# A gMLP trunk on one core: the second block's x is transposed by DMA in 16-bit planes, weights are asked for a unit sooner, and TensorE runs on the identity at the start

## Chip, core and metric

The kernel runs on one core of a Trainium2 chip. The metric is the device time in microseconds (us) of one execution, given as the median of three runs. The core's engines each have their own queue of instructions and meet through semaphores: TensorE (PE in the profile; its weight loads are PEld), VectorE (DVE), ScalarE (ACT), GpSimd (POOL) and SyncE (SP), which issues all DMAs of this kernel.

## The reference

One layer of the reference is used (DEPTH 1, so the chunked gMLP). x is 2048 rows of 1024 (T and D_MODEL), E is 2048, all float32:

```python
c_act = jax.nn.silu(c)
mod = c_act @ ada_w[0] + ada_b[0]
shift, scale, gate = jnp.split(mod, 3, axis=-1)
h = rmsnorm(x, norm_g[0]) * (1.0 + scale[:, None, :]) + shift[:, None, :]
u, v, z = jnp.split(h @ w_in, 3, axis=-1)
u = jax.nn.gelu(u)
v = layernorm(jax.nn.gelu(v), ln_g, ln_b)
v = v.reshape(bsz, seq // 128, 128, 8, 256)
v = jnp.einsum("hpq,bnqhc->bnphc", sp_w, v) + sp_b.T[None, None, :, :, None]
y = (u * v.reshape(bsz, seq, 2048) * jax.nn.silu(z)) @ w_out
x = x + gate[:, None, :] * y
return rmsnorm(x, final_g)
```

## The kernel before

**Products.** Each float32 product is made of three fp32r matmuls (`mm3`, L177): an operand is split into a high part (`hi`, `sh`; a cast on ScalarE, L168) and a low part (`lo`, `sl`; what is left, a subtraction on VectorE, L169), and hi*hi, hi*lo and lo*hi are summed in PSUM. The large products go by a scheme of Strassen's kind with seven products (p1 to p7) of half the size, from sums of quarters: S1 to S4 of h (`strassen_sums`), and differences of the weights' quarters (`Unit.weights`, L342), which VectorE makes in place in the raw weights (`sub`, L345).

**Stages.** The rows of x are worked in two blocks of 1024. For each block v is made first (groups of 4 row tiles, `project_v`), then the 16 units, u and z in turn, of 256 columns each (`project`, L957). A unit's raw weights are 1 MB in the single buffer `raw0` (u) or `raw1` (z), loaded by `Unit.load` (L298). A unit's products are twelve matmuls of 128x512 each. `after` (L938) is the work on a unit's results one unit later: the spatial mixing (`pmix`), the products of u, v and z, stores to `g_dram`.

**The start** (L723 on) computes the modulation from c (`mod_sum`: a sum on VectorE, then `pm` on TensorE), loads the first 512 rows of x as four chunks of 128, normalises each (`normalize_steps`: square on ScalarE, a small row `r_m` on VectorE, a power on GpSimd, a scaling `x<-x,r` on VectorE) and transposes it on TensorE against the identity (`psx`, L269). Then come the first products, step k by step k of the 1024 (`p` from L806 on), of weights wfv and wfu; for each k `modulate` (L252) and `put` make sh and sl.

**The second block's x** is prepared beside block 0, a tile of 128 rows at a time (`prepare_h`, L659), in 8 tiles: load into the one buffer `hx`, normalise, transpose on TensorE into PSUM (`psh`, 8 transposes of 128x128 a tile, 64 in all), modulate on ScalarE into `ht`, store to `h_dram`. `preparations` (L854) hands out these steps, one at each hook of `project_v` or two in each unit; `side` (L908) starts the second block's sums (`prepare_sums`: from h_dram to hs_dram) in units 6, 8, 10 and 12. `refill` (L692) loads both at the turn of the blocks.

**Order.** A scheduler orders the instructions of TensorE, GpSimd and SyncE by its own estimate; in the start the order of VectorE and ScalarE is as written. All DMAs stand in one queue on SyncE, which issues in order: one that waits for its buffer holds all behind it. c tiles (2 KB a partition) come from a pool of 15.

Of the kernel before, what the change touches and what calls it, by code (L numbers as in the profile page):

```python
# [9 lines left out]
F32 = mybir.dt.float32  # L10
F32R = mybir.dt.float32r
BF16 = mybir.dt.bfloat16
AF = mybir.ActivationFunctionType
ALU = mybir.AluOpType
PSUM = bass.MemoryType.PSUM
# [2 lines left out]
P = 128  # L18
# [4 lines left out]
def kernel(  # L23
# [33 lines left out]
    nc = tc.nc  # L57

    T, D = x.shape
# [6 lines left out]
    KD = D // P  # L66
# [591 lines left out]

    def prepare_h(tp):  # L659

        xt = vp.tile([P, D], F32, tag="hx", name=f"x_1_{tp}", bufs=1)
        t0 = TB + tp * P
        nc.sync.dma_start(xt, x[t0:t0 + P, :])
        yield
        normalize_x(xt, f"1_{tp}")
        yield
        for i in range(KD // 4):
            ps = aux_bank(f"psh_{tp}_{i}")
            ht = c_tile(f"ht_{tp}_{i}", (P, 4, P))
            for kk in range(4):  # L670
                k = 4 * i + kk
                nc.tensor.transpose(ps[:, kk * P:(kk + 1) * P], xt[:, k * P:(k + 1) * P], ident)
            for kk in range(4):
                modulate(ht[:, kk, :], ps[:, kk * P:(kk + 1) * P], 4 * i + kk)
            nc.sync.dma_start(h_dram[:, 4 * i:4 * i + 4, tp * P:(tp + 1) * P], ht)
        yield

    def prepare_sums(k):
# [44 lines left out]
    with tc.tile_pool(name="start", bufs=1) as st:  # L723
# [22 lines left out]
        firsts = [units[2 * j] for j in range(NF)]  # L746
        v0, v1 = groups[0]

        def take_a1(k):
            ps = transpose_half(xh, 0, k, acc_bank if k < 5 else aux_bank)  # L750
            t = s_slot(S4, k % KH, "hl"[k // KH], F32, f"a1_{k}")
            if k == 0:
                modulate(t, ps, k)
            elif k in (1, 3):
                nc.vector.tensor_copy(t, ps)
            else:
                nc.scalar.activation(t, ps, AF.Copy)
            a1.append(t)

        with tc.manual_schedule(engines={mybir.EngineType.DVE, mybir.EngineType.Activation}):  # L760
            *_, pm[0] = mod_sum(0, aws[0])
            mod_cols(cols, 0, pm[0])
            sums = mod_sum(1, aws[1])
            for ch, xt in enumerate(xh):
                norm = normalize_steps(xt, f"0_{ch}")
                next(norm)
                pm[1] = next(sums)
                next(norm)
            ws = [first_split(k, wf[k]) for k in range(2)]
            for k in range(5):  # L770
                take_a1(k)
                if k == 0:
                    put(0, A11, 0, a1[0])
            for k in range(KD):
                if k + 3 < KD:
                    aws[k + 3] = mod_load(st, k + 3)
# [77 lines left out]
    def preparations():  # L854

        ln = prepare_ln()
        next(ln)
        sp = [prepare_spatial(g) for g in range(2)]
        next(sp[0])
        yield  # L860
        next(ln, None)
        next(sp[0])
        next(sp[1])
        yield
        next(sp[0], None)
        next(sp[1])
        yield
        next(sp[1], None)
        hs = [prepare_h(tp) for tp in range(NCH)]
        next(hs[0])  # L870
        yield
        for tp in range(1, NCH + 1):
            next(hs[tp - 1])
            yield
            next(hs[tp - 1])
            if tp < NCH:
                next(hs[tp])
            yield
# [29 lines left out]
    def side(i):  # L908

        next(prep, None)  # L910
        if i in (6, 8, 10, 12):
            prepare_sums((6, 8, 10, 12).index(i))
        if 0 <= i - NU < KD:
            for db in range(NDB):
                prepare_gate(NDB * (i - NU) + db, gate_sum)
# [41 lines left out]
    def project(i, u, rest):  # L957
# [10 lines left out]
        if turn:  # L968
            w0.load(0, 0, "raw0")
            w0.load(0, 1, "v0")  # L970
        if i % NU:
            u.load()
            u.p1()
            change(A11)
            u.p5()
# [391 lines left out]
```

## Time and profile before

| what | value |
|---|---|
| median of 3 runs | 1337.66 us (1336.67 to 1340.08) |
| the profiled execution | 1340.57 us, span 1338.7 us |
| TensorE busy | 1310.6 us, 98%, 6078 matmuls and transposes |
| VectorE busy | 1077.9 us, 81% |
| ScalarE busy | 683.9 us, 51% |
| GpSimd busy | 26.3 us, 2% |
| DMA | 229.23 MB, mean 171 GB/s |

The span is the time between the first and the last instruction of the profiled execution; its own time is 1.9 us longer. A row of a timeline gives the start, the length, the engine, the line and the operation, with out<-in by the program's names; in brackets stands how long the engine had been idle and what released it. Matmuls are pipelined, so the time that one takes from TensorE is the step from its start to the next one's start, not its length. The clock granted to TensorE has two levels, 1.2 and 2.4 GHz.

### The profile page before, as it was taken

What the parts mean: (1) busy time and instruction counts of PE and PEld (TensorE: products, weight loads), DVE (VectorE), ACT (ScalarE), POOL (GpSimd) and SP (SyncE); (2) the same over time, 40 slices, a digit from 0 to 9 for tenths busy, and PEclk for the clock granted to TensorE, in tenths of its full rate; (3) what the DMA queues carried; (4) which work ended last, traced back from release to release, by engine and by line L of the source; (5) the groups of instructions that cost most, each with busy time, mean ns of one, the idle gap of its engine ahead of it and who ended that gap; (6) DMA issues with size and microseconds to landing.
All of it is one profiled execution on the core that took longest, in us unless ns stands there. A gap on an engine that the chain in (4) does not pass through costs nothing.

```text
span 1338.7 us, 17246 instructions
## 1 busy us (share of the span) xinstructions
PE 1310.6 (98%) x6078; PEld 1089.7 (81%) x6078; DVE 1077.9 (81%) x1801; ACT 683.9 (51%) x1177; POOL 26.3 (2%) x42
## 2 busy tenths in 40 slices
PE   5999999999999999999999999999999999999997
PEld 4878887878788888888888888888888888888886
DVE  6889988878889888977687889887799944757875
ACT  5775444757655546634345555445543434344553
POOL 0000001000000000000000000000000000000101
PEclk9999999999999999999999999999999999999999
DMA  9871655546566448532242445334338722235733
GB/s 317 265 268 63 221 190 196 162 159 214 192 217 216 166 140 289 197 129 107 95 157 91 157 153 185 133 120 133 123 118 305 268 95 94 95 119 204 259 110 126
DMA packets 156798, 229.23 MB, mean 171 GB/s; under 512 B 9188, under 2 KB 91172, under 8 KB 153384
## 3 DMA queue, kind: packets, MB, share of 16 engines
q1 hardware_dynamic: 156712, 228.14, 50.1%
q8 instruction: 47, 0.77, 0.2%
q14 instruction: 39, 0.32, 0.1%
HBM read 160.47 MB, written 67.64 MB: 170 GB/s over the span
## 4 chain that ended last, share of the span: by engine, by line
PE 89%; DVE 4%; DMA 3%; issue 1%; ACT 1%; POOL 0%; SPq 0%; POOLq 0%; DVEq 0%; ACTq 0%
PE po L178 8%; PE po L180 8%; PE po L179 8%; PE p_z L180 7%; PE p_z L178 7%; PE p_z L179 7%; PE p_u L178 6%; PE p_u L180 6%; PE p_u L179 6%; PE p_v L178 6%; PE p_v L180 6%; PE p_v L179 6%; PE pmix_u L557 4%; DMA raw_u<-in_gm_w_in_dram 2%; PE p L180 1%
## 5 line engine op out<-in xcount | busy, mean ns | idle before, releaser
L178 PE MATMUL p_v<-hi_p_v,sh 128*128 128x512 f32 x416 | 162.5, 391 | 1.6 <-DVE u_v L485 1.0
L179 PE MATMUL p_v<-lo_p_v,sh 128*128 128x512 f32 x416 | 162.3, 390 | 0.0
L180 PE MATMUL p_v<-hi_p_v,sl 128*128 128x512 f32 x416 | 162.2, 391 | 0.0
L180 PE MATMUL po<-hi_o,gl 128*128 128x512 f32 x416 | 161.9, 389 | 0.0
L178 PE MATMUL po<-hi_o,gh 128*128 128x512 f32 x416 | 161.8, 389 | 0.0
L179 PE MATMUL po<-lo_o,gh 128*128 128x512 f32 x416 | 161.8, 389 | 0.0
L168 ACT ACTIVATE hi_p_v<-b_v 128x512 fp32r<-128x512 f32 x104 | 65.2, 631 | 108.4 <-PE p_v L180 87.7
L168 ACT ACTIVATE gh<-gr 128x1024 fp32r<-128x1024 f32 x52 | 55.1, 1061 | 127.0 <-PE po L179 117.4
L169 DVE TENSOR_TENSOR gl<-gr,gh 128x1024 fp32r<-128x1024 f32 x52 | 63.9, 1228 | 59.3 <-ACT gh L168 59.1
L169 DVE TENSOR_TENSOR lo_p_v<-b_v,hi_p_v 128x512 fp32r<-128x512 f32 x104 | 70.2, 690 | 35.9 <-ACT hi_p_v L168 35.7
L178 PEld LDWEIGHTS p_v<-hi_p_v,sh 128*128 128x128 f32 x416 | 78.1, 188 | 19.3 <-DVE u_v L485 1.9
L180 PEld LDWEIGHTS po<-hi_o,gl 128*128 128x128 f32 x416 | 78.1, 188 | 16.6 <-DVE gl L169 0.3
L178 PEld LDWEIGHTS po<-hi_o,gh 128*128 128x128 f32 x416 | 78.1, 188 | 16.1
L179 PEld LDWEIGHTS p_v<-lo_p_v,sh 128*128 128x128 f32 x416 | 78.1, 188 | 16.1 <-DVE lo_p_v L169 0.2
L179 PEld LDWEIGHTS po<-lo_o,gh 128*128 128x128 f32 x416 | 78.1, 188 | 16.1
L180 PEld LDWEIGHTS p_v<-hi_p_v,sl 128*128 128x128 f32 x416 | 78.1, 188 | 16.0
L542 ACT ACTIVATE vn<-vn,lm,lr 128x256 f32<-128x256 f32 x128 | 67.9, 594 | 24.1 <-DMA vn<-v_dram 18.8
L180 PE MATMUL p_z<-sh,lo_p_z 128*128 128x512 f32 x192 | 75.9, 396 | 2.1 <-DVE lo_p_z L169 2.0
L178 PE MATMUL p_z<-sh,hi_p_z 128*128 128x512 f32 x192 | 75.5, 393 | 1.0 <-ACT hi_p_z L168 1.0
L179 PE MATMUL p_u<-sl,hi_p_u 128*128 128x512 f32 x196 | 76.3, 389 | 0.0
L178 PE MATMUL p_u<-sh,hi_p_u 128*128 128x512 f32 x196 | 76.2, 389 | 0.0
L180 PE MATMUL p_u<-sh,lo_p_u 128*128 128x512 f32 x196 | 76.2, 389 | 0.0
(244 smaller groups left out, 3103.1 us busy)
## 6 DMA issues: line engine op xcount, KB each, us to landing
gr<-g_dram SPq DMA_DIRECT2D x26, 1024.0 KB, 4.7
b_v<-in_gm_w_in_dram SPq DMA_DIRECT2D x18, 1024.0 KB, 7.5
vn<-v_dram SPq DMA_DIRECT2D x16, 1024.0 KB, 6.1
raw_u<-in_gm_w_in_dram SPq DMA_DIRECT2D x16, 1024.0 KB, 6.1
raw_z<-in_gm_w_in_dram SPq DMA_DIRECT2D x16, 1024.0 KB, 5.2
v_dram<-c_v SPq DMA_DIRECT2D x44, 256.0 KB, 2.1
g_dram<-c_u SPq DMA_DIRECT2D x37, 256.0 KB, 2.5
aw<-in_ada_w_dram SPq DMA_DIRECT2D x16, 512.0 KB, 5.3
```

Of the source, the lines that this page charges most:

```text
L168: nc.scalar.activation(hi, src, AF.Copy)
L169: nc.vector.tensor_tensor(lo, src, hi.bitcast(F32), op=ALU.subtract)
L178: nc.tensor.matmul(ps, lhsT=sh, rhs=mh, start=first, stop=False)
L179: nc.tensor.matmul(ps, lhsT=sh, rhs=ml, start=False, stop=False)
L180: nc.tensor.matmul(ps, lhsT=sl, rhs=mh, start=False, stop=last)
L542: nc.scalar.activation(vt[:, ch, :], vt[:, ch, :], AF.Identity, bias=lm[:, ch:ch + 1], scale=lr[:, ch:ch + 1],)
L557: nc.tensor.matmul(pm[:, i * P:(i + 1) * P], lhsT=vt[:, m * (NCH // 2) + i, f * P:(f + 1) * P], rhs=spT[:, u.j, :], start=True, stop=True,)
```

## The change

1. In the start TensorE multiplies the identity by itself into a bank that nobody reads (`spun`): 20 times ahead of the first `pm`, then 16, 3, 3 and 0 times ahead of the four chunks, and 6 times after the last. TensorE's order in this part is as written now.
2. In `prepare_h` ScalarE writes the normalised x tile as two planes of 16-bit words (the low and the high halves of each float32). SyncE issues two transposing DMAs, from plane to `turned`. GpSimd copies the turned halves back into the x tile, in words of every second place, so that it holds the transposed x. ScalarE modulates it in place (8 rows of 128x128), and one DMA of 512 KB stores it. A tile takes three steps instead of two, and the x tile is occupied until its store has read it.
3. `prepare_sums` runs in units 10 to 13.
4. `project` calls `load` of the next unit at its beginning, where a unit called its own.

```diff
 def prepare_h(tp):
     ...
     normalize_x(xt, f"1_{tp}")
+    planes, turned = [], []
+    for i in range(2):
+        planes.append(c_tile(f"plane_{tp}_{i}", (P, D), U16))
+        nc.scalar.activation(planes[i], xt.bitcast(U16)[:, i::2], AF.Copy)
     yield
-    for i in range(KD // 4):
-        ps = aux_bank(f"psh_{tp}_{i}")
-        ht = c_tile(f"ht_{tp}_{i}", (P, 4, P))
-        for kk in range(4):
-            k = 4 * i + kk
-            nc.tensor.transpose(ps[:, kk * P:(kk + 1) * P], xt[:, k * P:(k + 1) * P], ident)
-        for kk in range(4):
-            modulate(ht[:, kk, :], ps[:, kk * P:(kk + 1) * P], 4 * i + kk)
-        nc.sync.dma_start(h_dram[:, 4 * i:4 * i + 4, tp * P:(tp + 1) * P], ht)
+    for i in range(2):
+        turned.append(c_tile(f"turned_{tp}_{i}", (P, KD, P), U16))
+        nc.sync.dma_start_transpose(turned[i], planes[i])
+    yield
+    ht = xt.rearrange("p (k t) -> p k t", t=P)
+    for i in range(2):
+        nc.gpsimd.tensor_copy(ht.bitcast(U16)[:, :, i::2], turned[i])
+    for k in range(KD):
+        modulate(ht[:, k, :], ht[:, k, :], k)
+    nc.sync.dma_start(h_dram[:, :, tp * P:(tp + 1) * P], ht)
     yield
...
+        spun = acc_bank("spun")
+        def spin(n):
+            for _ in range(n):
+                nc.tensor.matmul(spun[:, :P], lhsT=ident, rhs=ident, start=True, stop=True)
...
+        with tc.manual_schedule(engines=written | {mybir.EngineType.PE}):
+            spin(20)
             *_, pm[0] = mod_sum(0, aws[0])
...
+            psx = [acc_bank(f"psx_0_{k}") for k in range(5)]
             for ch, xt in enumerate(xh):
+                spin((16, 3, 3, 0)[ch])
...
+                for k in range(5):
+                    nc.tensor.transpose(
+                        psx[k][:, ch * P:(ch + 1) * P], xt[:, k * P:(k + 1) * P], ident
+                    )
+            spin(6)
...
-        if i in (6, 8, 10, 12):
-            prepare_sums((6, 8, 10, 12).index(i))
+        if 10 <= i < 10 + KH:
+            prepare_sums(i - 10)
...
+        if i % NU < NU - 1:
+            units[i + 1].load()
         if i % NU:
-            u.load()
             u.p1()
```

What stands where on the engines, at three places. In the lists x3 stands for three like rows, and the number at a name's end is that of its buffer.

TensorE at the start, from the transpose of the modulation's rows (`ps_rows`) to the second chunk's first `psx`; before:

```order
L733 MATMUL ps_rows<-ident,rows 128x32
L235 MATMUL pm_226<-ones,am_216 128x1 x2
L269 MATMUL psx_0_293<-ident,x_0_191 128x128
L269 MATMUL psx_1_304<-ident,x_0_191 128x128
L269 MATMUL psx_2_311<-ident,x_0_191 128x128
L269 MATMUL psx_3_318<-ident,x_0_191 128x128
L269 MATMUL psx_4_325<-ident,x_0_191 128x128
L269 MATMUL psx_0_293<-ident,x_1_193 128x128
```

The same place after the change:

```order
L740 MATMUL ps_rows<-ident,rows 128x32
L761 MATMUL spun<-ident 128x128 x20
L236 MATMUL pm_247<-ones,am_237 128x1 x2
L761 MATMUL spun<-ident 128x128 x16
L789 MATMUL psx_0_253<-ident,x_0_191 128x128
L789 MATMUL psx_1_254<-ident,x_0_191 128x128
L789 MATMUL psx_2_255<-ident,x_0_191 128x128
L789 MATMUL psx_3_256<-ident,x_0_191 128x128
L789 MATMUL psx_4_257<-ident,x_0_191 128x128
L761 MATMUL spun<-ident 128x128 x3
L789 MATMUL psx_0_253<-ident,x_1_193 128x128
```

The order of the transposes is the same; between them stand the products on the identity.

VectorE in the unit z at some 270 us, from its first low part of p (`lo_p_0_z`); `raw_u` is the next u unit's raw weights, whose load the subtractions wait for, and `r_3_m` and `x_3` belong to a tile of the second block's x. Before:

```order
L169 TENSOR_TENSOR lo_p_0_z_2766<-raw_z_2762,hi_p_0_z_2765 128x512
L345 TENSOR_TENSOR raw_z_2762<-raw_z_2762 128x4x128
L320 TENSOR_TENSOR c_0_u_2673<-p_0_u_2660,u_0_u_2651 128x512
L345 TENSOR_TENSOR raw_z_2762<-raw_z_2762 128x4x128
L345 TENSOR_TENSOR raw_u_2979<-raw_u_2979 128x4x128 x2
L320 TENSOR_TENSOR u_0_u_2651<-p_0_u_2706,u_0_u_2651 128x512
L320 TENSOR_TENSOR c_0_u_2611<-p_0_u_2706,c_0_u_2611 128x512
L320 TENSOR_TENSOR c_0_u_2611<-p_0_u_2727,c_0_u_2611 128x512
L149 TENSOR_SCALAR r_3_m<-ss_3_2753 128x1
L160 TENSOR_SCALAR x_3_2700<-x_3_2700,r_3_2755 128x1024
L169 TENSOR_TENSOR lo_p_0_z_2785<-raw_z_2762,hi_p_0_z_2784 128x512
```

After:

```order
L170 TENSOR_TENSOR lo_p_0_z_2786<-raw_z_2636,hi_p_0_z_2785 128x512
L346 TENSOR_TENSOR raw_z_2636<-raw_z_2636 128x4x128 x2
L321 TENSOR_TENSOR u_0_u_2678<-p_0_u_2722,u_0_u_2678 128x512
L321 TENSOR_TENSOR c_0_u_2638<-p_0_u_2722,c_0_u_2638 128x512
L170 TENSOR_TENSOR lo_p_0_z_2805<-raw_z_2636,hi_p_0_z_2804 128x512
L346 TENSOR_TENSOR raw_u_2782<-raw_u_2782 128x4x128
L346 TENSOR_TENSOR raw_z_2636<-raw_z_2636 128x4x128
L321 TENSOR_TENSOR c_0_u_2638<-p_0_u_2743,c_0_u_2638 128x512
L346 TENSOR_TENSOR raw_u_2782<-raw_u_2782 128x4x128
```

The second low part of p stands ahead of both subtractions of raw_u now, and the rows on the x tile are no longer between.

ScalarE one unit earlier, around the second tile of the second block's x, where `vn` are rows of the normalised v; before:

```order
L168 ACTIVATE hi_b_0_u_2656<-raw_u_2609 128x512
L317 ACTIVATE u_0_z_2451<-u_0_z_2451 128x512
L157 ACTIVATE sq_2_2570,ss_2_2571<-x_2_2513 128x1024
L168 ACTIVATE hi_t_0_u_2702<-raw_u_2609 128x512
L317 ACTIVATE c_0_z_2394<-c_0_z_2394 128x512
L542 ACTIVATE vn_2_2948<-vn_2_2948,lm,lr 128x256
L168 ACTIVATE hi_t_0_u_2723<-raw_u_2609 128x512
L542 ACTIVATE vn_2_2948<-vn_2_2948,lm,lr 128x256 x4
L168 ACTIVATE hi_p_0_z_2765<-raw_z_2762 128x512
```

After:

```order
L671 ACTIVATE plane_1_2544<-x_1_2237 128x1024
L169 ACTIVATE hi_b_0_u_2683<-raw_u_2435 128x512
L318 ACTIVATE u_0_z_2494<-u_0_z_2494 128x512
L169 ACTIVATE hi_t_0_u_2718<-raw_u_2435 128x512
L318 ACTIVATE c_0_z_2437<-c_0_z_2437 128x512
L543 ACTIVATE vn_2_2953<-vn_2_2953,lm,lr 128x256
L169 ACTIVATE hi_t_0_u_2739<-raw_u_2435 128x512
L543 ACTIVATE vn_2_2953<-vn_2_2953,lm,lr 128x256 x4
L254 ACTIVATE x_1_2237<-x_1_2237,mshift,mscale 128x128 x8
L169 ACTIVATE hi_p_0_z_2785<-raw_z_2636 128x512
```

Between the tile's planes and its eight modulations stand the rows from `hi_b_0_u` to the fifth `vn`; the high part of z's p stands behind the modulations.

## Rows read from the trace of the kernel before

**Rows 1.** The page: busy time by engine, and the chain that ended last.
```profile
PE 1310.6 (98%) x6078; PEld 1089.7 (81%) x6078; DVE 1077.9 (81%) x1801; ACT 683.9 (51%) x1177; POOL 26.3 (2%) x42
...
PE 89%; DVE 4%; DMA 3%; issue 1%; ACT 1%; POOL 0%; SPq 0%; POOLq 0%; DVEq 0%; ACTq 0%
```
**Rows 2.** Timeline of TensorE in the start: start, length, row, [idle, releaser].
```profile
15.47 1.33 PE L269 MATMUL psx<-ident,x 128*128 128x128 f32 x5 [3.65 <-DVE r_m L149]
...
22.61 0.80 PE L178 MATMUL p<-hi_wfv,sh 128*128 128x512 f32 x1 [0.68 <-ACT sh L168]
...
27.90 0.51 PE L178 MATMUL p<-sh,hi_wfu 128*128 128x512 f32 x1
...
30.15 0.48 PE L178 MATMUL p<-hi_wfv,sh 128*128 128x512 f32 x1
```
**Rows 3.** Timeline of ScalarE in the same stretch.
```profile
25.51 0.91 ACT L225 ACTIVATE am<-aw,c_act 128x256 f32<-128x256 f32 x2 [1.19 <-DMA aw<-in_ada_w_dram]
...
27.16 0.63 ACT L168 ACTIVATE sh<-a 128x512 fp32r<-128x512 f32 x1
```
**Rows 4.** Timeline of VectorE in the same stretch.
```profile
13.47 0.15 DVE L149 TENSOR_SCALAR r_m<-ss 128x1 f32<-128x1 f32 x1 [1.13 <-ACT sq L157]
...
28.41 0.69 DVE L169 TENSOR_TENSOR sl<-a,sh 128x512 fp32r<-128x512 f32 x1
```
**Rows 5.** Timeline of TensorE around the first group of transposes, and one later.
```profile
193.82 0.39 PE L178 MATMUL p_v<-hi_p_v,sh 128*128 128x512 f32 x1
...
195.18 1.03 PE L672 MATMUL psh<-ident,x 128*128 128x128 f32 x8
...
196.29 0.40 PE L179 MATMUL p_v<-lo_p_v,sh 128*128 128x512 f32 x1
...
247.76 0.66 PE L672 MATMUL psh<-ident,x 128*128 128x128 f32 x4 [0.22 <-DVE t_u L563]
```
**Rows 6.** All rows of the tile psh on TensorE: ns min/median/max, first and last.
```profile
L672 PE MATMUL psh<-ident,x x64: 270/272/328, 195.2 to 368.5; 128*128 128x128 f32 x64
```
**Rows 7.** Timeline of TensorE around 277 us.
```profile
274.34 0.39 PE L180 MATMUL p_z<-sh,lo_p_z 128*128 128x512 f32 x1
...
277.46 0.79 PE L180 MATMUL p_z<-sh,lo_p_z 128*128 128x512 f32 x1 [0.95 <-DVE lo_p_z L169]
...
280.91 0.39 PE L179 MATMUL p_z<-sl,hi_p_z 128*128 128x512 f32 x1
```
**Rows 8.** VectorE ahead of it, and its waits for raw_u: total, times, longest.
```profile
271.44 1.42 DVE L345 TENSOR_TENSOR raw_u<-raw_u 128x512 f32<-128x512 f32 x2 [2.85 <-DMA raw_u<-in_gm_w_in_dram]
...
DVE raw_u L345 <- DMA raw_u<-in_gm_w_in_dram: 6.4, 4, 2.8
```
**Rows 9.** SyncE's queue: the issue of that load.
```profile
263.09 0.38 SPq L301 DMA_DIRECT2D raw_u<-in_gm_w_in_dram  x1
```
**Rows 10.** Busy time by engine from 225 to 450 us: PE, PEld, DVE, ACT, POOL.
```profile
225.00:450.00 225.00, 221.67 (x1085) 184.92 (x1084) 186.21 (x305) 137.92 (x254) 6.91 (x8) 0.99 0.57 185
```
**Rows 11.** Groups of ScalarE: busy time and mean ns of one.
```profile
L253 ACT ACTIVATE ht<-psh,mshift,mscale 128x128 f32<-128x128 f32 x64 | 23.5, 459 | 0.0
L157 ACT ACTIVATE sq<-x 128x1024 bf16<-128x1024 f32 x16 | 16.7, 1048 | 9.6 <-DMA x<-in_x_dram 9.5
```
**Rows 12.** DMA issues: queue, count, KB of one, us from issue to landing.
```profile
v_dram<-c_v SPq DMA_DIRECT2D x44, 256.0 KB, 2.1
...
hq<-h_dram SPq DMA_DIRECT2D x16, 256.0 KB, 6.5
```
**Rows 13.** Groups of GpSimd: busy time and mean ns of one.
```profile
masks.py:199 POOL TENSOR_SCALAR_AFFINE_SELECT ident<-ident 128x128 f32<-128x128 f32 x1 | 0.3, 294 | 0.1
masks.py:197 POOL MEMSET ident<- 128x128 f32 x1 | 0.2, 205 | 0.3 <-POOLq L1346 0.3
```
**Rows 14.** Timeline of ScalarE around the second tile.
```profile
253.75 0.63 ACT L168 ACTIVATE hi_b_u<-raw_u 128x512 fp32r<-128x512 f32 x1 [1.58 <-PE p_z L179]
...
264.21 0.63 ACT L168 ACTIVATE hi_p_z<-raw_z 128x512 fp32r<-128x512 f32 x1
```

More of the change, by code (lines that the diff above doesn't have):

```diff
@@ L12 @@
 BF16 = mybir.dt.bfloat16
+U16 = mybir.dt.uint16
 AF = mybir.ActivationFunctionType
@@ L747, with take_a1 @@
         v0, v1 = groups[0]
-        def take_a1(k):
-            ps = transpose_half(xh, 0, k, acc_bank if k < 5 else aux_bank)
+        spun = acc_bank("spun")
+        def spin(n):
+            for _ in range(n):
+                nc.tensor.matmul(spun[:, :P], lhsT=ident, rhs=ident, start=True, stop=True)
+        def take_a1(k, ps=None):
+            if ps is None:
+                ps = transpose_half(xh, 0, k, aux_bank)
             t = s_slot(S4, k % KH, "hl"[k // KH], F32, f"a1_{k}")
@@ L758, in take_a1 @@
             a1.append(t)
-        with tc.manual_schedule(engines={mybir.EngineType.DVE, mybir.EngineType.Activation}):
+        written = {mybir.EngineType.DVE, mybir.EngineType.Activation}
+        with tc.manual_schedule(engines=written | {mybir.EngineType.PE}):
+            spin(20)
             *_, pm[0] = mod_sum(0, aws[0])
@@ L768 @@
                 next(norm)
+                for k in range(5):
[3 more added lines that the diff above has]
+            spin(6)
             ws = [first_split(k, wf[k]) for k in range(2)]
             for k in range(5):
-                take_a1(k)
+                take_a1(k, psx[k])
                 if k == 0:
                     put(0, A11, 0, a1[0])
+        with tc.manual_schedule(engines=written):
             for k in range(KD):
@@ L872, in preparations @@
         for tp in range(1, NCH + 1):
-            next(hs[tp - 1])
-            yield
+            for _ in range(2):
+                next(hs[tp - 1])
+                yield
             next(hs[tp - 1])
```

## Prediction

> **What bounds the kernel now.** I read the busy shares and the chain of work that ended last first: TensorE (PE) is busy for 98% of the span and the chain runs through it for 89% [rows 1]. So an edit is worth what it takes off TensorE's own row of work, or off the stretches in which TensorE stands still or runs at the lower clock; time saved on another engine is worth nothing by itself. Three places matter, and I read the timeline of each. First the start, up to the second group of products: [rows 2] is TensorE, [rows 3] ScalarE (ACT), [rows 4] VectorE (DVE). Then the 64 transposes of the second block's x [rows 5, 6]. Then the longest stall of the middle, around 277 us [rows 7 to 9]. Last I looked at how much room the other engines have in the stretch from 225 to 450 us, in which the new steps come to lie [rows 10].
>
> I sum against the profiled execution, 1340.57 us (span 1338.7 us and 1.9 us around it). It is 2.9 us above the median of 1337.66 us, so 2.9 us come off at the end. About 0.3% (4.0 us) is what a measurement of this kernel can tell from no change.
>
> **The transposes leave TensorE: 7.1 us less.** The profile shows 64 [rows 6], in 12 groups among the products. Ahead of the first group six products take from 193.82 to 195.18, a step of 0.227 us [rows 5]. From the first of its eight transposes at 195.18 to the second product behind them at 196.29 are 1.11 us, of which one product's step is 0.23: 0.88 us for a group of eight; there are four such. Read in the same way, of the eight groups of four, four cost 0.33 and three 0.45 us. The last costs 0.89 us, since its transposes waited for a buffer: 247.76, 0.22 us of them for DVE [rows 5]. Sum 4 x 0.88 + 4 x 0.33 + 3 x 0.45 + 0.89 = 7.1 us. All of it lay on TensorE's own row, so it goes whole.
>
> **The start at full clock: 1.9 us less, between 2.6 less and 0.6 more.** Twelve products start between 22.61 and 27.90 [rows 2]: 5.29 us, where 12 x 0.227 = 2.72 would do. So 2.6 us are lost to the lower level (1.2 instead of 2.4 GHz), after idle time between the four chunks of transposes (3.65 us ahead of the first of them [rows 2]). The change fills this time with 48 small products on the identity. They wait for nothing but the identity, and TensorE has no work of its own there; what they delay is pm_0, which DVE then uses, and DVE idles 1.13 us before its next row at 13.47 [rows 4], so a delay of up to 1.1 us is covered. If the clock is up at 22.6, the first group ends 2.6 us sooner, but the second can't follow at once: ScalarE waits 1.19 us for the weights of the modulation, and its sh of the second group starts only at 27.16 [rows 3], 0.63 us long; VectorE's sl of the same starts at 28.41 [rows 4]. The second group began at 30.15 [rows 2]. It can start with sh at about 27.8 on four of its products (4 x 0.227 = 0.9) and then needs sl at 29.1, so it starts in effect at 28.2: 30.15 - 28.2 = 1.9 us gained. If the clock stays low, the six spins behind the last transposes take some 0.22 us each, 1.3 us, against 0.68 us of idle time ahead of the first product [rows 2]: 0.6 us lost. Here, as everywhere below, the higher level is what the step of 0.227 shows, and the lower the step of 5.29/12 = 0.44.
>
> **Weights asked for sooner, and the rows of VectorE in another order: 4.1 us less, between 0 and 5.** From the product at 274.34 to the one at 280.91 stand 11 products [rows 7]: 6.57 us, where 11 x 0.227 = 2.50 would do. 4.1 us are lost, to two waits (0.95 us of one are shown) and to the lower clock after them. The releaser is VectorE's lo_p_z, and VectorE was late since it stood 2.85 us at the subtraction of raw_u until 271.44, for a load [rows 8] that SyncE issued at 263.09 [rows 9]. The load is asked for earlier in the program now, but its single buffer comes free with the same subtraction as before, so I expect it at about the same time. What helps is the order: the second lo_p_z of this unit now stands ahead of the first subtraction of raw_u, where it stood six rows behind both before. Then a late load holds nothing that TensorE needs in the next 2 us. VectorE waits for raw_u four times, 6.4 us in all [rows 8]; the other three cost little, and at least one keeps its place. I take the 4.1 us, 0 as one end (a new stall of the same size elsewhere), 5 as the other.
>
> **The casts into planes and the modulation on ScalarE: nothing.** 16 casts of 128x1024, nearest row the square of the same size, 1.048 us [rows 11]: 16.8 us. They lie on an engine that works 138 of 225 us in this stretch [rows 10]. The 64 modulations stay (0.459 us each [rows 11]) and read SBUF, not PSUM; I price this the same. Without this room the casts would cost their 16.8 us.
>
> **The transposing DMAs and GpSimd's copies: 4 us more, between 0 and 17.** No row shows a transposing DMA. A plain store of the same 256 KB lands in 2.1 us, a slow load in 6.5 us [rows 12]. No row shows a copy on GpSimd: ScalarE takes 1.05 us for 128x1024 [rows 11], GpSimd itself 0.205 us for a fill and 0.294 for a select of 128x128 [rows 13], eight times which is 1.6 and 2.4 us. I take 1.6 us, 16 copies make 26 us. GpSimd is idle otherwise, so the copies cost nothing by their own length. They cost where they come late for ScalarE's modulations, and where they take something from VectorE. How late: between the plane of the second tile and its modulations stand rows of ScalarE that in the trace run from hi_b_u (253.75) to hi_p_z (264.21) [rows 14], so 10.5 us. Issue, two transfers that overlap and two copies make 0.7 + 2.1 + 3.2 = 6 us at the low end and 0.7 + 2 x 6.5 + 3.2 = 17 us at the high end. I take about 10, near the store, since source and target are SBUF: in time for most of the eight tiles. What they take from VectorE: it works 186 of 225 us here [rows 10], so 83% of the 26 us, 21 us, meet VectorE at work. If each meeting held it for its whole length and TensorE lost 0.8 us for each of VectorE's (the stall above and its like: some 5.2 of 6.4 us), that would be 17 us. But VectorE has 39 us of idle time here, so most holds would be caught up; I take a quarter of 17, 4 us.
>
> SyncE's queue gets 16 transposes and gives up half of the 16 stores of h (one 512 KB store a tile instead of two); the load of the next x tile now waits for this store, and 3 steps a tile instead of 2 leave time for it. The sums of the second block move four to two units back, with their loads and stores; nobody needs them before the turn of the blocks. Both at nothing. If that cover is gone, a 6.5 us load would be late once, not each time.
>
> **Sum.** 1340.57 - 7.1 - 1.9 - 4.1 + 4 = 1331.5 us against the profiled execution, less 2.9: 1328.6, say **1328.5 us**.
>
> **Rivals.**
>
> *GpSimd's copies hold VectorE (same time as before).* For it: VectorE is at work for 83% of the stretch, and stalls of TensorE there come from VectorE [rows 7]. Against it: 39 us of idle time. Price: between 9 and 17 instead of 4, which is 1333.5 to 1341.5; middle 1337.5. Chance 0.17.
> The Trainium skill has a rule for this ("SBUF — State Buffer", Who interferes with whom): GpSimd shares a pair of ports with VectorE, the pair is locked for a whole instruction, and a VectorE row with both inputs in SBUF blocks fully against a GpSimd row that reads SBUF. Every hi/lo subtraction and every subtraction of raw weights is such a row. No run here shows it yet; by this rule the time is this rival's.
>
> *The transposed tile comes late (slower).* ScalarE works in order, so a modulation that waits holds every hi part behind it, and TensorE with it. TensorE has some 5.5 us of products in hand there (two products of units, 12 x 0.227 = 2.7 us each), so it decides at 10.5 + 5.5 = 16 us from plane to modulation, and each us over that costs one us per tile. At 18 us: 8 x 2 = 16 us, 1344.5; at 25 us, 8 x 9 = 72 us, 1400. For it: two serial transfers like the slow load already come to 17 us, the queue of SyncE stands still behind a long issue, and nothing in the trace bounds a transposing DMA from above. Against it: the stores of the same 256 KB land in 2.1 us [rows 12]. Chance 0.15, mostly near the low end.
> The Trainium skill gives an effective rate of 261 GB/s for transposing DMAs ("DMA: Bandwidth & Descriptors", Latency and other measured facts), by which one plane would take an estimated 1.0 us and this rival would fall away. The trace has no row for it.
>
> *The change doesn't do what it says.* The load is not sooner since the buffer isn't, and the stall comes back in another place; and the 48 spins don't raise the clock, as the 20 transposes didn't. Each alone: 1332.6 and 1331.0; both: 1328.5 + 4.1 + 2.5 = 1335.1. Chance 0.18, half of it within 0.3%.
>
> **How the numbers follow.** The forecast itself has 0.50. Below 1333.65 (faster by over 0.3%) lie the forecast, half of the last rival and 0.03 of the first: 0.62. Above 1341.7 lie 0.13 of the late tile and 0.04 of the held VectorE: 0.17. Within lies the rest, 0.21. The range: low 1321, where nothing is lost to the copies (-4), the start gives 2.6 (-0.7), VectorE's order 5 (-0.9) and one more stall of some 2 us goes; high 1343, which takes in the held VectorE whole and the first part of the late tile. It leaves out about 0.05 below and 0.13 above.
>
> **What would show it.** Right: no group of transposes among the products after 195 us, so 7 us less of TensorE's work; products at a step of 0.23 us from 22 us on, the second group near 28.2; no stall near 265 us, where the same products now fall; GpSimd's copies near 1.6 us and VectorE's rows as long as before. Wrong: VectorE's subtractions of 0.69 us grow where a copy runs (first rival), TensorE or ScalarE waits for a modulation whose releaser is GpSimd or a DMA (second), products at 0.43 us at the start or VectorE waiting for raw_u ahead of a lo part (third).

## The result: 1353.0 us, slower by 1.05%

The changed kernel takes 1353.0 us (median of 4 runs, 1350.6 to 1353.6) where the kernel before took 1338.9 us beside it; the ratio is 1.0105 with a 95% interval of 1.009 to 1.012. The forecast was 1328.5 us, faster, with a range to 1343.

From the page of the changed kernel, the rows that answer to [rows 1], then the waits of TensorE and of ScalarE (for whom, total us, times, longest):

```profile
PE 1318.5 (98%) x6110; PEld 1095.6 (81%) x6110; DVE 1086.2 (80%) x1801; ACT 699.6 (52%) x1193; POOL 53.1 (4%) x58
...
PE 65%; DVE 2%; issue 1%; ACT 1%; POOL 0%; POOLq 0%; DVEq 0%; ACTq 0%
```

```profile
PE p_z L179 <- ACT hi_p_z L169: 9.7, 2, 5.3
PE p_u L179 <- ACT hi_p_u L169: 3.7, 1, 3.7
...
PE pmix_u L558 <- DVE t_u L564: 1.6, 1, 1.6
PE p_u L179 <- ACT hi_t_u L169: 1.4, 1, 1.4
...
ACT x L254 <- POOL x L679: 21.1, 7, 6.4
...
ACT sq L158 <- DMA x<-in_x_dram: 18.5, 5, 8.7
```

TensorE's three longest waits beyond the start are for high parts made by ScalarE; the next, 1.55 us at 409 us, is for VectorE's `t_u`. ScalarE's new waits are for the second block's x: 21.1 us at the modulations (behind GpSimd's copies) and 18.5 us at the squares (behind the load of the next tile; [rows 11] had 9.5 us there, 8.5 us of it in the start, where it is 8.7 us now). The 1.55 us come from the same chain: a square stands 3.80 us for its load, VectorE's `u_z` then waits 2.56 us for a row of ScalarE that stands behind the casts, and `t_u` comes three rows later.

Where the time went can be read by counting products. Both kernels make 5372 products of 512 columns; the table sets the start of the n-th in one trace against the other.

| product | before, us | after, us | difference |
|---|---|---|---|
| 0 | 22.61 | 22.52 | -0.1 |
| 24 | 31.62 | 29.99 | -1.6 |
| 720 | 200.60 | 198.10 | -2.5 |
| 1056 | 291.39 | 282.62 | -8.8 |
| 1176 | 321.74 | 321.88 | +0.1 |
| 1320 | 361.33 | 364.39 | +3.1 |
| 1560 | 423.90 | 434.40 | +10.5 |
| 5160 | 1280.88 | 1292.73 | +11.9 |

By the 1056th product the changed kernel has gained 8.8 us: 1.6 us in the start, about half of the 7.1 us of the transposes (32 of the 64 lie before it), and the 4.1 us of the stall at 274 us, of which a wait of 0.33 us is left. That this is near the -9.1 us of the sum is luck: half of the transposes was still to come off, and nothing had been paid for what replaced them. Then five stalls cost 23.8 us: at 299 (1.7 us), 309 (7.8), 356 (6.1), 409 (1.7) and 423 us (6.5). About 17 us of this is waiting, 6.5 us are products at the low clock behind the waits; the granted clock is 0.79 and 0.86 in windows around the three long ones.

**One stall in rows.** Changed kernel, fifth tile, in the order of the chain: SyncE, GpSimd, ScalarE, then TensorE waiting for the last high part.

```profile
344.35 6.89 SPq L675 DMA_TRANSPOSE turned<-plane  x2
...
352.57 3.53 POOL L679 COPY x<-turned 128x1024 uint16<-128x1024 uint16 x2 [14.57 <-issue]
...
348.19 0.61 ACT L169 ACTIVATE hi_p_z<-raw_z 128x512 fp32r<-128x512 f32 x1
352.03 0.64 ACT L318 ACTIVATE u_u<-u_u 128x512 f32<-128x512 f32 x1 [3.23 <-DVE u_u L321]
356.13 0.88 ACT L254 ACTIVATE x<-x,mshift,mscale 128x128 f32<-128x128 f32 x2 [3.47 <-POOL x L679]
356.92 0.61 ACT L318 ACTIVATE c_u<-c_u 128x512 f32<-128x512 f32 x1
357.44 2.40 ACT L254 ACTIVATE x<-x,mshift,mscale 128x128 f32<-128x128 f32 x6
359.74 0.57 ACT L378 ACTIVATE c_z<-p_z 128x512 f32<-128x512 f32 x1
360.22 0.62 ACT L169 ACTIVATE hi_p_z<-raw_z 128x512 fp32r<-128x512 f32 x1
```

The planes were ready at 340.8. The two transposes occupy SyncE until 351.2, the copies GpSimd until 356.1. ScalarE is free at 352.7 and stands 3.47 us before the modulations. Then come its own rows, 4.1 us, and only then the high part that TensorE has wanted since 356.5. TensorE starts at 360.89, after an idle time of 4.40 us, and runs its next eight products at the low clock. Without the wait of 3.47 us it would still have been some 0.9 us late.

The other kind of stall, the fourth tile: the load of x waits for the store of the tile before, since both use one buffer.

```profile
300.35 0.55 SPq L682 DMA_DIRECT2D h_dram<-x  x1
...
303.67 0.33 SPq L665 DMA_DIRECT2D x<-in_x_dram  x1
...
308.78 1.06 ACT L158 ACTIVATE sq<-x 128x1024 bf16<-128x1024 f32 x1 [2.48 <-DMA x<-in_x_dram]
...
309.95 1.28 ACT L318 ACT_TABLE_LOAD   x1
311.24 0.63 ACT L318 ACTIVATE c_u<-c_u 128x512 f32<-128x512 f32 x1
311.78 1.99 ACT L671 ACTIVATE plane<-x 128x1024 uint16<-128x1024 uint16 x2
313.67 0.61 ACT L318 ACTIVATE u_u<-u_u 128x512 f32<-128x512 f32 x1
314.19 0.61 ACT L169 ACTIVATE hi_p_z<-raw_z 128x512 fp32r<-128x512 f32 x1
...
314.85 0.80 PE L179 MATMUL p_z<-sh,hi_p_z 128*128 128x512 f32 x1 [5.28 <-ACT hi_p_z L169]
```

ScalarE waits 2.48 us for the load, and then square, table load, both casts and two functions stand ahead of the high part: TensorE waits 5.28 us.

### The profile page after: what moved, and what is told of

Read it like the earlier page. It is cut to its first block, busy times and chain, and to the rows that moved or that the text cites. A ratio compares the mean times of both kernels' runs of the same rounds, so it can differ in the third digit from the quotient of the medians.

```text
span 1350.5 us, 17362 instructions
## 1 busy us (share of the span) xinstructions
PE 1318.5 (98%) x6110; PEld 1095.6 (81%) x6110; DVE 1086.2 (80%) x1801; ACT 699.6 (52%) x1193; POOL 53.1 (4%) x58
## 4 chain that ended last, share of the span: by engine, by line
PE 65%; DVE 2%; issue 1%; ACT 1%; POOL 0%; POOLq 0%; DVEq 0%; ACTq 0%
PE po L181 7%; PE po L180 7%; PE po L179 7%; PE p_z L180 5%; PE p_z L179 5%; PE p_z L181 5%; PE p_u L179 5%; PE p_u L180 5%; PE p_u L181 5%; PE p_v L180 4%; PE p_v L181 4%; PE p_v L179 4%; PE pmix_u L558 3%; DVE gl L170 0%; DVE c L1185 0%
## 5 line engine op out<-in xcount | busy, mean ns | idle before, releaser
L180 PEld LDWEIGHTS po<-lo_o,gh 128*128 128x128 f32 x416 | 78.1, 188 | 16.4
L181 PEld LDWEIGHTS p_v<-hi_p_v,sl 128*128 128x128 f32 x416 | 78.1, 188 | 15.9
```

The source lines that it names most:

```text
L180: nc.tensor.matmul(ps, lhsT=sh, rhs=ml, start=False, stop=False)
L181: nc.tensor.matmul(ps, lhsT=sl, rhs=mh, start=False, stop=last)
```

## The experiments

Ratios are to the kernel before on the same chip. Three theories were set against each other. **A**: the tile comes late, and ScalarE, in order, holds the high parts. **B**: GpSimd's copies hold VectorE. **C** was first that the moved loads collide; it fell with the first four runs, and the letter then stands for: the place of the waiting rows in ScalarE's order decides.

### Which part of the change

**The start alone** (the new start in the kernel before). 

> The kernel before with the new start alone (products on the identity, TensorE's order as written there). All theories: the second group of products begins near 28.5 us instead of 30.15 us and nothing else moves, so 1.5 to 2 us less, about 0.999 of before. If the start moved the later order, the loss of 14 us would show here already: 1.005 or more.

Measured: 1334.9 us, ratio 0.998 (0.9966 to 0.9994). The second group of products begins at 28.67. About as expected. Its profile also lacks the stall at 274 us, though nothing there was changed: TensorE's idle time in the stage from the 768th to the 1700th product is 0.3 us, where the profiled execution of before has 3.3 us.

**The sooner loads alone** (the line `units[i + 1].load()`). 

> The kernel before with the loads of raw weights one unit sooner in the program, alone. Theory A (the loss is ScalarE held in order by the late x tile): no loss, 0 to 4 us less than before, the stall at 274 us smaller or gone. Rival C (the moved loads collide with other transfers and VectorE waits for them): 5 us or more slower, TensorE waiting for VectorE behind raw_u or raw_z.

Measured: 1338.1 us, ratio 1.0012 (1.0001 to 1.0023). No gain and no loss to speak of. SyncE issues the load of raw_u ahead of the stall at 263.05 us, where it was 263.09 [rows 9], and the order of VectorE's rows around it is as before. The stall is there, if smaller: VectorE waits 2.12 us for raw_u, TensorE 0.34 and 0.95 us, and the clock stays up behind them. The collision falls.

**The DMA transposes and later sums alone.** 

> The kernel before with the DMA transposes of the second block's x and the later sums alone. Theory A (late tile): the whole loss is here, 12 to 20 us slower than before (1.009 to 1.015), TensorE waiting 3 to 6 us at a time for ScalarE's hi parts that stand behind a modulation or a square of x. Rival C (moved loads): within 4 us of before.

Measured: 1352.6 us, ratio 1.0115 (1.010 to 1.013): the whole loss. TensorE waits 5.3, 5.9 and 4.1 us for ScalarE at 307, 354 and 422 us. In the stretch of these stalls ScalarE's order is that of the changed kernel row by row. The later sums were not tried alone, but they also stand in e6_own_tile below, which has no loss.

**Start and loads, transposes on TensorE.** 

> The changed kernel with the transposes back on TensorE (new start and sooner loads alone). Theory A: 2 to 6 us faster than before (0.996 to 0.999). Rival C: slower than before by 5 us or more.

Measured: 1336.0 us, ratio 0.9987 (0.9977 to 0.9997), 1.7 us less, a little under what A said, and no loss.

### What makes the transposes dear

**The modulations on GpSimd.**

```diff
-            modulate(ht[:, k, :], ht[:, k, :], k)
+            nc.gpsimd.tensor_scalar(ht[:, k, :], ht[:, k, :], mscale[:, k:k + 1],
+                mshift[:, k:k + 1], op0=ALU.mult, op1=ALU.add)
```

> The changed kernel with the 64 modulations of the second block's x on GpSimd instead of ScalarE, so that ScalarE waits for no copy. Theory A (ScalarE in order, held by the late tile): TensorE's stalls behind a modulation (299, 356 and 423 us, 14 us with the low clock after them) go, those behind a square of x that waits for its load (309 and 409 us, 9 us) stay, since the tile is free no sooner: 1337 to 1345 us. Theory B (GpSimd's copies hold VectorE, and that is the loss): GpSimd reads SBUF longer now, so VectorE's rows of two SBUF inputs are stretched more often: 1353 us or more.

Measured: 1369.3 us, ratio 1.023. That is 24 us above the range for theory A. ScalarE no longer waits for a modulation, but SyncE does. GpSimd, SyncE and ScalarE in this kernel:

```profile
300.36 6.71 POOL L681 TENSOR_SCALAR x<-x,mscale,mshift 128x128 f32<-128x128 f32 x8
...
291.75 0.33 SPq L576 DMA_DIRECT2D g_dram<-c_z  x1
307.10 0.56 SPq L685 DMA_DIRECT2D h_dram<-x  x1
307.70 0.67 SPq L375 DMA_DIRECT2D c_u<-c_dram  x1
308.47 0.59 SPq L541 DMA_DIRECT2D vn<-v_dram  x1
...
316.09 2.56 ACT L543 ACTIVATE vn<-vn,lm,lr 128x256 f32<-128x256 f32 x5 [15.26 <-DMA vn<-v_dram]
...
319.23 0.80 PE L179 MATMUL p_z<-sh,hi_p_z 128*128 128x512 f32 x1 [9.12 <-ACT hi_p_z L169]
```

The store of the tile stands 15 us at the head of SyncE's queue, the load of vn behind it comes late, ScalarE waits 15.26 us for that load, and TensorE 9.12 us for the high part behind it. The wait moved to another queue in order and cost more: theory A in kind, not in the number. It doesn't decide against B, since GpSimd works more here.

**Tiles of their own for the turned x**, so that the x tile is free once its planes are cast.

```diff
-    ht = xt.rearrange("p (k t) -> p k t", t=P)
+    for g in range(2):
+        ht = c_tile(f"ht_{tp}_{g}", (P, 4, P))
...
+        nc.sync.dma_start(h_dram[:, 4 * g:4 * g + 4, tp * P:(tp + 1) * P], ht)
```

> The changed kernel with the turned x copied into tiles of its own (two of 128x4x128, stored by one DMA each, as before), so that the x tile is free for the next load once its planes are cast. Theory A: the stalls behind the square of x (309 and 409 us, 9 us) go, those behind the modulations (14 us) stay: 1341 to 1347 us. Theory B: no change, 1350 to 1355 us.

Measured: 1334.2 us, ratio 0.9977 (0.9959 to 0.9994), 19 us less than the changed kernel and more than I expected. The waits at the squares go (10.0 us are left, 8.6 of them in the start): the next tile is loaded while the last is still being turned. Those at the modulations shrink from 21.1 to 3.0 us too, but not because a tile is turned sooner: from planes to turned tile it takes 11.4 us in the mean, as in the changed kernel (11.5), and 15.9 and 17.0 us in the third and the seventh. The modulations stand further back in ScalarE's order: it reaches those of the third tile 16.4 us after the planes instead of 9.7, those of the seventh 15.1 instead of 9.2, and doesn't wait there. GpSimd copies as many bytes as before, VectorE's rows beside the copies take 9.0 us longer in all (10.8 in the changed kernel), and the loss is gone: B is not the loss.

**Plain DMAs** in place of the transposing ones. 

> The changed kernel with plain DMAs from plane to turned in place of the transposing ones, so x is not transposed (this part of the computation is left out); bytes, casts, copies and modulations stay. Theory A: an issue takes SyncE 0.3 to 0.6 us instead of 2.6 us and the tile is there about 5 us sooner, so nearly all stalls go: 1328 to 1338 us. Theory B: the copies hold VectorE as before, 1348 us or more.

Measured: 1338.5 us, ratio 1.0001 (0.9986 to 1.0016), half a us above the range for A. All DMAs of the tile turned, in the changed kernel and in this one (ns min/median/max of the issue):

```profile
L675 SPq DMA_TRANSPOSE turned<-plane x16: 1248/2557/3674, 195.8 to 442.4; - x16
```

```profile
L675 SPq DMA_DIRECT2D turned<-plane x16: 484/546/1046, 195.5 to 427.6; - x16
```

From issue to landing both take 4.2 to 4.3 us in the median; the transposing one keeps SyncE 2 us longer. ScalarE's order is nearly that of the changed kernel (some 20 of 278 rows around the second block's x stand elsewhere), so this is the run closest to lateness alone: the third, fifth and seventh tile are turned 1.9 to 3.4 us sooner after their planes, and ScalarE's waits at the modulations fall from 21.1 to 10.7 us. The longer issue and the queue that it makes are worth 15 us here.

**The copies on VectorE** (`nc.vector.tensor_copy`). 

> The changed kernel with the copies of the turned planes on VectorE instead of GpSimd. Theory B: no hold any more, for 16 copies of about 1 us on VectorE itself: 1330 to 1342 us. Theory A: the transposes are as late as before, and now VectorE, in order too, waits for them as well: 1350 us or more.

Measured: 1336.5 us, ratio 0.9989 (0.9977 to 1.0002). The number is B's. A's number is missed by over 13 us. But a copy takes 0.75 us instead of 1.75, so the tile is also some 2 us sooner, which A gains from as well; ScalarE's waits at the modulations fall to 9.0 us. By itself it doesn't tell A from B.

**Each copy of GpSimd twice.**

```diff
         nc.gpsimd.tensor_copy(ht.bitcast(U16)[:, :, i::2], turned[i])
+    for i in range(2):
+        nc.gpsimd.tensor_copy(planes[i], turned[i].rearrange("p k t -> p (k t)"))
```

> The changed kernel with every copy of GpSimd doubled: behind the two that ScalarE waits for, two more of the same size go from turned into the planes, which nobody reads. They meet VectorE's rows as the first do. Theory A: 1351 to 1357 us, since the tile is as early as before. Theory B (what costs is GpSimd holding VectorE): VectorE loses another 10 us of its time, most of which TensorE shows: 1360 us or more.

Measured: 1347.4 us, ratio 1.0062 (1.0041 to 1.0083): 5.6 us less than the changed kernel. VectorE loses 15.9 us by the copies instead of 10.8, and the kernel is faster: together with the tiles of their own, which keep the hold and lose the loss, B falls as the cause. What the added hold itself costs can't be read off, since the order changed too (below). But A had no gain to offer either: from planes to turned tile it takes 12.4 us in the mean of the eight tiles, against 11.5 in the changed kernel. ScalarE's order differs, though: the scheduler, which reckons with the doubled copies, has put a high part ahead of the fourth tile's square.

```profile
306.46 0.63 ACT L169 ACTIVATE hi_p_z<-raw_z 128x512 fp32r<-128x512 f32 x1 [1.05 <-DVE raw_z L346]
307.38 1.06 ACT L158 ACTIVATE sq<-x 128x1024 bf16<-128x1024 f32 x1 [0.29 <-DMA x<-in_x_dram]
```

The stall of 7.8 us that the changed kernel has here is a wait of 0.64 us (the square also waits 0.29 us for its load instead of 2.48). So one stall that went makes up for more than the whole gain.

### Lateness or place

**The transposes one step sooner**, in the step of the casts, with an empty step behind.

```diff
             nc.scalar.activation(planes[i], xt.bitcast(U16)[:, i::2], AF.Copy)
-        yield
         for i in range(2):
             turned.append(c_tile(f"turned_{tp}_{i}", (P, KD, P), U16))
             nc.sync.dma_start_transpose(turned[i], planes[i])
         yield
+        yield
```

> The changed kernel with the two transposing DMAs in the step of the casts, one step sooner in the program; period and order of steps stay. Theory A (lateness alone): SyncE reaches them up to 4 us sooner in the tiles where they queued (third, fifth and seventh), so 1336 to 1345 us. Theory C (the place of ScalarE's rows decides): the modulations move ahead in ScalarE's order by as much as the scheduler thinks the tile is sooner, and wait as long as before: 1347 us or more.

Measured: 1335.7 us, ratio 0.998 (0.9968 to 0.9993), just under the range for A. The transposes no longer stand in SyncE's queue behind loads and stores that wait: from planes to turned tile it takes 4.9 to 7.0 us instead of 5.6 to 15.9. That is worth 17 us, but it is not lateness alone. The modulations have moved ahead in ScalarE's order, as theory C said, and ScalarE still waits long for them, 17.8 us instead of 21.1 (here with the seventh tile's modulations and the next high part for a product):

```profile
ACT x L254 <- POOL x L679: 17.8, 8, 3.4
```

```profile
397.94 3.19 ACT L254 ACTIVATE x<-x,mshift,mscale 128x128 f32<-128x128 f32 x8 [3.42 <-POOL x L679]
...
402.98 0.61 ACT L169 ACTIVATE hi_p_u<-raw_u 128x512 fp32r<-128x512 f32 x1
```

TensorE waits for no high part behind the third, fifth or seventh tile's modulations. A wait of 3.42 us of ScalarE costs it nothing here, where one of 3.47 us in the changed kernel's fifth tile was followed by 4.40 us of TensorE's: so the place counts. TensorE's one long wait left, 4.1 us at 308 us, is behind the fourth tile's square and casts.

**One of the two calls for the preparation earlier in the unit** (`if n == 0` for `if n == 1`). 

> The changed kernel with one of a unit's two calls for the preparation behind the first instead of the second part of its work: nothing is shortened, but in ScalarE's order a hi part of z now stands between the fourth tile's square and its casts, where both stood ahead of it before. Theory A: within 3 us of the changed kernel. Theory C: the stall at 309 us (7.8 us) shrinks, 1343 to 1350 us.

Measured: 1339.8 us, ratio 1.0011 (0.9997 to 1.0024): 13 us less, more than either theory said. From planes to turned tile it takes 11.1 us in the mean, as in the changed kernel (11.5), but the mean hides a shift between the tiles: the third, fifth and seventh come 3 to 4 us sooner than there, the second and sixth 4 us later. ScalarE around the fourth tile:

```profile
304.26 1.06 ACT L158 ACTIVATE sq<-x 128x1024 bf16<-128x1024 f32 x1 [0.68 <-DMA x<-in_x_dram]
...
305.98 0.63 ACT L169 ACTIVATE hi_p_z<-raw_z 128x512 fp32r<-128x512 f32 x1 [0.57 <-DVE raw_z L346]
308.57 2.01 ACT L671 ACTIVATE plane<-x 128x1024 uint16<-128x1024 uint16 x2 [1.95 <-DVE x L161]
```

With the high part between square and casts, TensorE's wait here is 3.30 us instead of 5.28; but the square waits 0.68 us for its load instead of 2.48, and the other stalls shrink with tiles that are less late. So this run doesn't tell place from lateness. For the three other tiles that stalled TensorE in the changed kernel, each cell has the way from planes to turned tile, ScalarE's wait at the modulations, and TensorE's wait for the high part behind them, in us:

| version | third tile | fifth | seventh |
|---|---|---|---|
| changed kernel | 15.9, 6.2, 1.4 | 15.3, 3.5, 4.4 | 15.5, 6.4, 3.7 |
| plain DMAs | 12.5, 2.6, 0 | 13.3, 2.6, 2.8 | 12.5, 2.7, 0 |
| transposes sooner | 4.9, 3.4, 0 | 5.4, 1.4, 0 | 4.9, 3.4, 0 |
| one call earlier | 12.5, 4.1, 0.7 | 12.2, 2.7, 1.7 | 11.6, 3.2, 1.2 |
| tiles of their own | 15.9, 0, 0 | 12.7, 3.0, 0.5 | 17.0, 0, 0 |

So both matter: the loss is made of a tile that is late for its place in ScalarE's order, and of high parts right behind that place. Being sooner helps where the order hardly changes (plain DMAs), and a way just as long costs nothing where the modulations stand further back (tiles of their own). No run splits the 17 to 19 us between the two.

### Towards a faster kernel

**Own tiles, old place of the loads** (start and transposes changed, loads not). 

> The changed kernel with the turned x in tiles of its own (as in e6_own_tile) and the loads of raw weights where they stood before. Theory A (the loss was the one x tile's cycle): the loss is away as in e6_own_tile, 1330 to 1336 us; the moved loads are worth nothing by e2_loads, so this is within 3 us of e6_own_tile. If the moved loads are what saves e6_own_tile: 1340 us or more.

Measured: 1335.2 us, ratio 0.9967 (0.9953 to 0.9981). The moved loads are not what saves e6_own_tile. This is the fastest ratio found, with intervals that overlap those of e1_start and e6_own_tile.

**Own tiles, copies on VectorE.** 

> The turned x in tiles of its own, and the copies on VectorE, which were e6_own_tile and e8_copy_dve: both theories expect the two gains to add in part, since e8 took VectorE's hold (11 us of its time) away and shortened the copies: 1328 to 1334 us. If VectorE, in order, waits for the transposing DMAs in its turn: 1336 us or more.

Measured: 1343.0 us, ratio 1.0035 (1.0022 to 1.0048): the two gains don't add; together they are 9 us slower than tiles of their own alone. At 262 us, VectorE makes the copies, and its next row is a low part for which it waits 4.30 us:

```profile
261.69 1.46 DVE L680 COPY ht<-turned 128x512 uint16<-128x512 uint16 x4
267.45 0.69 DVE L170 TENSOR_TENSOR lo_p_z<-raw_z,hi_p_z 128x512 fp32r<-128x512 f32 x1 [4.30 <-ACT hi_p_z L169]
```

VectorE waits once for a transposing DMA (3.7 us), and TensorE waits 3.6, 2.1 and 3.4 us for high parts at 271, 353 and 391 us. Why ScalarE's order is that much worse here was not traced further.

**The same without the moved loads.** 

> As e11_own_dve with the loads of raw weights where they stood before: within 3 us of e11_own_dve, 1328 to 1336 us.

Measured: 1343.5 us, ratio 1.0033 (1.002 to 1.0046), the same, and outside what I expected.

**Own tiles, copies and modulations one step later.** 

> As e9_no_loads (tiles of their own for the turned x, old place of the raw loads), with copies, modulations and stores of a tile one step later in the program, beside the next tile's casts. Theory A/C (the loss is what stands behind a late row in ScalarE's order): no modulation waits any more, TensorE's stalls of e9_no_loads at 272 and 387 us (some 7 us with the low clock) shrink: 1326 to 1333 us. If the copies' hold on VectorE or the busy ScalarE make those stalls: as e9_no_loads, 1334 to 1337 us.

Measured: 1336.1 us, ratio 0.9981 (0.9969 to 0.9992), no better than e9_no_loads. ScalarE waits for no modulation any more, and for no square's load after that of the first tile (2.1 us at 183 us), and yet TensorE waits 1.1, 2.3 and 1.3 us for high parts at 269, 307 and 384 us. ScalarE ahead of the second of these:

```profile
300.45 1.28 ACT L318 ACT_TABLE_LOAD   x1
301.75 0.63 ACT L318 ACTIVATE c_u<-c_u 128x512 f32<-128x512 f32 x1
302.29 3.18 ACT L254 ACTIVATE ht<-ht,mshift,mscale 128x128 f32<-128x128 f32 x8
305.37 1.04 ACT L158 ACTIVATE sq<-x 128x1024 bf16<-128x1024 f32 x1
...
307.19 0.63 ACT L318 ACTIVATE u_u<-u_u 128x512 f32<-128x512 f32 x1 [0.69 <-DVE u_u L321]
308.59 0.63 ACT L318 ACTIVATE c_u<-c_u 128x512 f32<-128x512 f32 x1 [0.77 <-DVE c_u L321]
309.12 0.61 ACT L169 ACTIVATE hi_p_z<-raw_z 128x512 fp32r<-128x512 f32 x1
```

Six microseconds of functions, modulations and a square stand in a row ahead of the high part, on an engine that is busy for little more than half of the time. VectorE waits 2.41 us for raw_u in the same place, so some of it is not the tile's. This bounds what the transposes' leaving TensorE is worth here: the stage from the 768th to the 1700th product takes 242.9 us in this profile, 243.3 us in that of e9_no_loads, and 240.7 us in that of e1_start, which still has 56 of the 64 transposes (6.2 us) in it.

## The prediction, step by step

**Transposes, -7.1 us: right as a removal, but it buys nothing.** The 64 are gone from TensorE's row. But what took the transposes' place (casts, blocks of modulations) costs as much in the best of the versions.

**Start, -1.9 us: right.** TensorE in the changed kernel, against [rows 2]:

```profile
21.26 1.50 PE L761 MATMUL spun<-ident 128*128 128x128 f32 x12
22.52 0.49 PE L179 MATMUL p<-hi_wfv,sh 128*128 128x512 f32 x1
...
25.66 0.39 PE L179 MATMUL p<-sh,hi_wfu 128*128 128x512 f32 x1
...
28.51 0.48 PE L179 MATMUL p<-hi_wfv,sh 128*128 128x512 f32 x1
```

Twelve products take 3.14 us instead of 5.29, and the second group begins at 28.51 instead of 30.15: 1.64 us gained; the new start alone measured 2.7 us less (0.8 to 4.5). The spins raised the clock where the 20 transposes with gaps had not. The bound by ScalarE's sh (27.17 now, 27.16 before) held.

**Loads and VectorE's order, -4.1 us: no sure gain.** The loads alone give nothing (1.0012); they are issued no sooner, as I said they might not be. In the changed kernel, with the order of VectorE that I foresaw, 0.33 us of the stall is left. But in the profiles of e1_start and of start and loads, with VectorE's order as before, TensorE doesn't wait there either: VectorE has raw_u 6.0 us after its issue, against 8.4 us in the kernel before and 7.6 in e2_loads, whose profile has the stall in part. So it comes and goes with the time that this load takes, and why that differs stays open, with one profile of each. I also took 2.9 us off because the profiled execution was that much above the median. If the stall was part of the 2.9, I counted it twice; that is not shown, since e2_loads has its waits in an execution 0.6 us below its median. And one of the stall's two waits, 1.04 us at 275.77, was for ScalarE's high part, where I named VectorE alone.

**Casts on ScalarE, nothing: wrong in part.** Their length is right (16 of 1.048 us). But I covered them with a mean share of 61%; in the rows they stand in a block with square, functions and modulations, ahead of a high part.

**Transposing DMAs and copies, +4 us, up to 17: the step that failed.** The term came to 23.8 us of stalls. Lengths were near: copies 1.75 us (1.6 taken), landing 4.3 us in the median and between 2.8 and 8.2 where the trace has it (my bounds were 2.1 and 6.5), 11.5 us from planes to turned tile in the mean (10 taken). What failed is the rival *The transposed tile comes late*, which I gave 0.15 and let begin at 16 us. The way took 5.6 to 15.9 us, never more, and the stalls still cost 23.8 us. The threshold had three faults. First, I gave TensorE 5.5 us of products in hand. In the fifth tile it had 3.8 us when ScalarE came free, and ScalarE's own rows (eight modulations and two functions, 4.1 us) and the high part (0.6 us) take more than that: it would have been late by some 0.9 us with no wait at all. Second, I looked only at the modulations. The x tile is in use until its store, so the next load, square and casts wait too; I wrote that three steps a tile leave time for that and put it at nothing. Third, I had no price for the low clock behind a stall, 6.5 us here.

**GpSimd holds VectorE: the mechanism is there, the loss is not.** GpSimd, then VectorE in the changed kernel:

```profile
316.16 3.45 POOL L679 COPY x<-turned 128x1024 uint16<-128x1024 uint16 x2 [5.42 <-DMA turned<-plane]
...
315.44 0.68 DVE L346 TENSOR_TENSOR raw_u<-raw_u 128x512 f32<-128x512 f32 x1
...
316.65 1.78 DVE L346 TENSOR_TENSOR raw_u<-raw_u 128x512 f32<-128x512 f32 x1
```

A subtraction with both inputs in SBUF takes 1.78 us beside a copy and 0.68 us otherwise. Over the 29 rows that meet a copy this is 10.8 us of VectorE, half of the 21 us that I set as the bound. Sums with one input in PSUM keep their 0.68 us. The Trainium skill's rule ("SBUF — State Buffer", Who interferes with whom) agrees in kind with these rows: who has two inputs in SBUF waits. But the rival's time (1337.5) is not what happened, and with 5 us more of such holds (e10_twice) the kernel is faster.

**The change doesn't do what it says:** true of the loads (issued at 263.05 us alone, at 263.09 before), not of the start.

## What to carry to other kernels

When work moves from the engine that bounds to a chain over three others, ask of each row in that chain not only whether its engine has idle time, but what stands behind it in that engine's order: a wait of 3.5 us on an engine that is little more than half busy stood ahead of a stall of 6.1 us here, because operands of the bounding engine were next in line. Free the source buffer at the first step that no longer needs it, and start the slow transfer in the step that makes its data; either alone brought back 17 to 19 us. And a stall seen in one profile is no gain to count on: look for it in a second one before it goes into a sum.

## What the runs showed of the hardware

- A transposing DMA of one 128x1024 plane of 16-bit words keeps SyncE for 2.56 us in the median of the changed kernel (1.25 to 3.67), a plain one of the same bytes in the same place for 0.55 us; from issue to landing both take about 4.3 us. Between these two the difference lies in the queue that issues. The 2.56 us are not fixed: issued one step sooner (e14_sooner), the 16 take 1.27 us in the median and land in 2.8 us.
- GpSimd's copy of 128x1024 16-bit words takes 1.34 us at the least and up to 3.05 us where VectorE's rows meet it; the hold goes both ways.
- GpSimd modulates a 128x128 tile in 0.77 us, where ScalarE takes 0.48 us from SBUF and took 0.46 us from PSUM.
- After idle times of 3.7 to 5.3 us in the changed kernel TensorE ran its next 8 to 12 products at a step of 0.43 us, the lower of the two levels.
